# The first pair of FFN1 in an order set by hand: x loaded ahead of the modulation's rows, and two shift columns computed on TensorE

## The chip, the cores and the metric

The kernel is one layer of a latent-token trunk and runs on one core of one Trainium2 chip. The metric is the device time of one execution in microseconds, as the median of several runs. "TensorE", "VectorE", "ScalarE" and "GpSimd" are PE, DVE, ACT and POOL in the profile's rows; SP is the engine whose queue issues nearly all of the DMAs.

## The reference, cut to what matters

The latent stream x (1024 tokens of 1024 channels) and a context stream (256 tokens) go through the same half-step SwiGLU FFN, each modulated by its own conditioning vector:

```python
cond_lat = jax.nn.silu(c)
cond_ctx = jax.nn.silu(c_ctx)[None, :]
m_l = jnp.split(cond_lat @ ada_w[i] + ada_b[i], N_MOD, axis=-1)      # 9 x 1024 columns
m_c = jnp.split(cond_ctx @ ada_w[i] + ada_b[i], N_MOD, axis=-1)
x = x + 0.5 * m_l[2][:, None, :] * swiglu(modulate(rms_norm(x, norm1_w[i]), m_l[0], m_l[1]),
                                          ffn1_w1[i], ffn1_w3[i], ffn1_w2[i])
ctx = ctx + 0.5 * m_c[2][:, None, :] * swiglu(modulate(rms_norm(ctx, norm1_w[i]), m_c[0], m_c[1]), ...)
# modulate(h, shift, scale) = h * (1 + scale) + shift;  swiglu(h) = (silu(h @ w1) * (h @ w3)) @ w2
```

After that come token mixing (retention and gated linear attention), a second half-step FFN and a last norm. All is done in 32-bit floats.

## The kernel before, in words

Channels lie on the 128 partitions: x is eight tiles `x{tg}{k}` of 128 channels by 512 tokens for each of two token groups tg 0 and 1. A 32-bit product is three TensorE matmuls of rounded parts (`mm3`, L62): `hi*hi` (L64), `hi*lo` (L65), `lo*hi` (L66), each 128x128 by 512 columns. The split into the parts is one pass on ScalarE (`hi`, L59) and one subtraction on VectorE or GpSimd (`lo`, L60).

**Modulation.** Column k of one of the nine groups (128 channels) is the dot product of 128 rows of the transposed `ada_w`, an `ada` tile of 128 x 1024 (512 KB), with the cond row, which lies on all partitions. `mod_col` (L101) loads the tile and has VectorE reduce it (L105), once for each stream wanted. A scale column gets `1 +` and the norm's weight in a 128x1 operation (L132). Group 0 is the shift and group 1 the scale of FFN1. There are three places for `ada` tiles (`AB = 3`), shared in turn.

**Norm.** `rstd` squares the eight x tiles on ScalarE, adds them on VectorE (`nacc`, L156), sums over channels on TensorE (L165) and takes the power -0.5 on GpSimd (`nr`, L912). Four diagonal matrices on VectorE (`ndiag`, L175) and four matmuls (L177) spread the result over partitions, and ScalarE copies it to `nrb` (L184). `norm_k` (L187) then makes for each k `nt = x * scale * nrb` on VectorE (L192), `hh` on ScalarE with the shift as bias (L193) and `hl` on VectorE (L194): the two parts of the modulated input.

**The first pair.** `first1` computes the hidden blocks f = 0 and 1 (w1 and w3: four weight columns i = 0 to 3) for both token groups while the norm and the modulation are still being made: stage st takes channel tile k = st of group 0 and k = st - LAG of group 1 (LAG = 4). Columns 2 and 3 of group 0 are held back until k = 3 (`LATE = 4`). In each stage `prep` issues the two modulation columns, the norm of that tile, some of the weights (`FIRST`), the loads of x for group 1 and, at k = 3, the norm's sum of group 1. The weights of this pair are split on ScalarE and GpSimd (eight GpSimd passes). All of this is written once in program order; a scheduler that weighs costs and priorities puts each engine's instructions into their final, fixed order.

**What follows.** Hidden blocks 2 and 3 (`classic_g`), then tiles `t1` to `t4` that are sums of the h tiles (L480 to L497, mostly VectorE), then the other blocks as chains of seven products (`hidden`). The remaining modulation columns are low-priority filler on VectorE (`mods`), each reduced once or twice (latent, context); the list `todo` holds them.

At the start the SP queue issues `cols` (biases and norm weights), the cond row, three `ada` rows, x0, a fourth `ada` row, then x1 to x7.

Of the kernel before, what the change touches and what calls it, by code (L numbers as in the profile page):

```python
# [30 lines left out]
class Trunk:  # L31
# [33 lines left out]
        mm(ps, wa[0], xa[1], start=False, stop=False, skip_group_check=more)  # L65
        mm(ps, wa[1], xa[0], start=False, stop=stop, skip_group_check=more)  # L66

    def consts(self, cond):
        nc, I, cp = self.nc, self.I, self.cp
        self.cols = self.tile(cp, [P, I["cols"].shape[1]], F32, "cols")  # L70
        nc.sync.dma_start(self.cols, I["cols"])
        cond()
# [4 lines left out]
        self.ident = self.tile(cp, [P, P], F32, "ident")  # L77
        self.pad(cp, 16)

    def cond(self):  # L80
        self.mod = [self.tile(self.cp, [P, 72], F32, "modl"), self.tile(self.cp, [P, 40], F32, "modc")]
# [12 lines left out]
    def ada_tile(self):  # L94
        self.ada += 1
        return self.tile(self.dp, [P, D], F32, f"ada{self.ada % AB}")

# [86 lines left out]
        self.nc.scalar.copy(rb[:, :n], pr)  # L184
        return rb[:, :n]

    def norm_k(self, tg, k, a, b, rb, pool, t=None):  # L187
        nc = self.nc
        n = TGS[tg][1]
        t = self.scr(pool, "nt")[:, :n] if t is None else t  # L190
        hi, lo = self.h[tg][k]
        nc.vector.scalar_tensor_tensor(out=t, in0=self.x[tg][k], scalar=a[:, k:k + 1], in1=rb, op0=ALU.mult, op1=ALU.mult)  # L192
        nc.scalar.activation(hi, t, AF.Identity, bias=b[:, k:k + 1])  # L193
        nc.vector.scalar_tensor_tensor(out=lo, in0=t, scalar=b[:, k:k + 1], in1=hi.bitcast(F32), op0=ALU.add,  # L194
                                       op1=ALU.subtract)
        return t

    def norm_t(self, tg, a, b, pool, tp):
# [406 lines left out]
    def first1(self, prep, ws):  # L605
        def first_k(pss, ids, tg, k):
            for i in ids:
                self.mm3(pss[i], self.wslice(ws[i], k), self.h[tg][k], k == 0, k == KD - 1)

        pss = {}  # L610
        prep(0, -1)
        for st in range(KD + LAG):
            if st == 0:
                pss[0] = [self.psA() for _ in range(4)]
            if st == LAG:
                pss[1] = [self.psB() for _ in range(4)]
            for tg, k in ((0, st), (1, st - LAG)):
                if not 0 <= k < KD:
                    continue
                prep(tg, k)  # L620
                late = LATE if tg == 0 else 0
                first_k(pss[tg], range(2) if k < late else range(4), tg, k)
                if k + 1 == late:
                    for kk in range(late):
                        first_k(pss[tg], range(2, 4), tg, kk)
# [635 lines left out]
    def run(self):  # L1261
        nc, tc, I = self.nc, self.tc, self.I
        S = {}

        def opn(name, side="left"):
            S[name] = tc.tile_pool(name=name, bufs=1, reuse_waits="tile", side=side)
            return S[name].__enter__()

        def cls(name):
            S[name].__exit__(None, None, None)  # L1270
# [4 lines left out]
        self.wp = opn("wp")  # L1275
        self.dp = opn("dp", "right")
        xp = opn("xp", "right")
        self.consts(lambda: self.cond())
        self.x, self.h, self.tr = {}, {}, None
        f1 = opn("f1")  # L1280
# [4 lines left out]
        for k in range(MK):  # L1285
            self.mod_col(8 + k, (0,), True)
            self.mod_col(k, (0,), True)
        self.load_x((xp, xp, None), (0,))
        nc.sync.dma_start(self.ident, self.I["ident"])
        self.alloc_h((0, 1), self.hp)  # L1290
        late = [self.tile(self.f1w, [P, D], F32R, f"w{i}") for i in range(1, 5)]
        late = [[(late[2 * i][:, o:o + 512], late[2 * i + 1][:, o:o + 512]) for o in (0, 512)] for i in range(2)]
# [7 lines left out]
        def prep(tg, k):  # L1300
            if k < 0:
                if tg == 0:
                    rb[0] = self.rstd(self.x[0], 512, n1)
                return
            if tg == 0 and k >= MK:
                self.mod_col(8 + k, (0,), True)
                self.mod_col(k, (0,), True)
            self.norm_k(tg, k, self.mcol(1), self.mcol(0), rb[tg], n1)
            if tg == 0:
                for i, q in FIRST.get(k, ()):  # L1310
                    load_first(i, q)
            if tg == 0 and XLK <= k < XLK + 4:
                self.load_x((xp, xp, None), (1,), (2 * (k - XLK), 2 * (k - XLK) + 1))
            if tg == 0 and k == RK:
                rb[1] = self.rstd(self.x[1], 512, n1)
# [21 lines left out]
        xp = opn("xp", "right")  # L1337
# [9 lines left out]
        for i, (tg, k) in enumerate((tg, 4 * q + k) for tg, q in ((0, 0), (1, 1), (0, 1), (1, 0)) for k in range(4)):  # L1347
            o = TGS[tg][0]
# [50 lines left out]
        A = self.bank4(self.psA)  # L1399
# [20 lines left out]
        xp = opn("xp", XS)  # L1420
        self.x = {}
        for tg in LATTG:
            o, n = TGS[tg]
# [25 lines left out]
        late = (None for _ in self.mods_half(f2, (8,)))  # L1449
# [21 lines left out]
MK = 2  # L1471
XLK = 0
RK = 3
LAG = 4
LR = (None, 60)
CRP = 0
VPRI = 100
# [1 line left out]
LATE = 4  # L1479
# [29 lines left out]
def layout(inputs):  # L1509
    g = {k: np.ascontiguousarray(v) for k, v in inputs.items()}  # L1510
    c = np.ascontiguousarray
    A = {}
# [2 lines left out]
    A["c"] = c(g["c"].reshape(1, D))  # L1515
    A["c_ctx"] = c(g["c_ctx"].reshape(1, D))
    A["adaT"] = c(g["ada_w"][0].T).reshape(72, P, D)

    def cols(v):
        return v.reshape(-1, P).T  # L1520
# [31 lines left out]
    j, i = np.arange(P)[:, None], np.arange(P)[None, :]  # L1552
# [30 lines left out]
```

## Time and profile before

| | us |
|---|---|
| median of 3 runs (lowest, highest) | 2210.6 (2210.41, 2212.17) |
| the profiled execution | 2213.09 |
| its span, first to last instruction | 2211.3 |
| TensorE busy in it | 2116.0 |
| VectorE busy in it | 1548.0 |
| ScalarE busy in it | 980.2 |
| GpSimd busy in it | 290.0 |
| first product of the pair starts | 31.55 |

The span is one execution as the profiler saw it, on one core; the profiled execution's own time is a little above it. Rows of the timeline give start, duration, engine, line, operation, what it writes and reads, and in brackets how long the engine had been idle and what ended that.

### The profile page before, as it was taken

The numbers are of one execution on the slowest core, as the hardware profiler recorded it, in microseconds if no ns is written. First come the engines' busy times: TensorE is split into PE (matmuls) and PEld (weight loads), VectorE is DVE, ScalarE is ACT, GpSimd is POOL, SyncE is SP. The second block draws the span as 40 slices with busy tenths as digits, with TensorE's granted clock in tenths as the row PEclk, the third lists the DMA queues.
The fourth block names the chain that finished last, engine by engine and source line by source line (L and its number), as shares of the span: only waits on it lengthen the run. The fifth ranks groups of instructions, "written<-read, shape, count | busy, mean of one in ns | idle before, by whom it ended". The sixth has DMA issues, their size and how long they took to land. (4 is left out here: it accounts for less than half of the span.)

```text
span 2211.3 us, 32718 instructions
## 1 busy us (share of the span) xinstructions
PE 2116.0 (96%) x11442; PEld 1796.9 (81%) x11442; DVE 1548.0 (70%) x2755; ACT 980.2 (44%) x1805; POOL 290.0 (13%) x294
## 2 busy tenths in 40 slices
PE   4999999999999999999989999899999999999998
PEld 3877888887788999887777988788878888888888
DVE  6999999765677755773666546767776767665676
ACT  3324343444454554555553435434344343444553
POOL 2000000000004655431032112200000000010000
PEclk9999999999999999999999999999999999999999
DMA  7548778458886565564222223325134444467674
GB/s 240 173 150 277 220 239 292 154 191 272 271 269 188 158 189 181 177 188 112 88 64 82 73 72 96 95 79 171 58 124 153 162 153 162 144 203 254 207 241 153
DMA packets 203079, 374.44 MB, mean 169 GB/s; under 512 B 23905, under 2 KB 37153, under 8 KB 202913
## 3 DMA queue, kind: packets, MB, share of 16 engines
q1 hardware_dynamic: 202912, 372.34, 52.8%
q8 instruction: 90, 1.47, 0.3%
q14 instruction: 77, 0.62, 0.1%
HBM read 297.76 MB, written 66.09 MB: 165 GB/s over the span
## 5 line engine op out<-in xcount | busy, mean ns | idle before, releaser
L59 ACT ACTIVATE whi<-raw 128x512 fp32r<-128x512 f32 (+1 forms) x659 | 406.3, 623 | 721.8 <-issue 198.8
L60 DVE TENSOR_TENSOR wlo<-raw,whi 128x512 fp32r<-128x512 f32 (+1 forms) x541 | 373.8, 694 | 310.7 <-ACT whi L59 308.2
L64 PE MATMUL psa<-hh,whi 128*128 128x512 f32 (+1 forms) x1476 | 544.6, 370 | 9.4 <-ACT hh L193 6.7
L65 PE MATMUL psa<-hl,whi 128*128 128x512 f32 (+1 forms) x1476 | 544.5, 369 | 1.2 <-DVE hl L60 0.7
L66 PE MATMUL psa<-hh,wlo 128*128 128x512 f32 (+1 forms) x1476 | 543.7, 368 | 1.8 <-DVE wlo L60 1.8
L64 PEld LDWEIGHTS psa<-hh,whi 128*128 128x128 f32 x1476 | 280.6, 190 | 55.4 <-ACT hh L193 7.9
L66 PEld LDWEIGHTS psa<-hh,wlo 128*128 128x128 f32 x1476 | 281.0, 190 | 45.2 <-DVE wlo L60 2.3
L65 PEld LDWEIGHTS psa<-hl,whi 128*128 128x128 f32 x1476 | 280.8, 190 | 45.3 <-DVE hl L60 1.8
L64 PE MATMUL psb<-hh,whi 128*128 128x512 f32 (+1 forms) x696 | 267.1, 385 | 4.7 <-ACT hh L59 2.5
L65 PE MATMUL psb<-hl,whi 128*128 128x512 f32 (+1 forms) x696 | 267.2, 384 | 1.8 <-DVE hl L60 1.8
L66 PE MATMUL psb<-hh,wlo 128*128 128x512 f32 (+1 forms) x696 | 266.7, 383 | 1.0 <-DVE wlo L60 1.0
L60 POOL TENSOR_TENSOR wlo<-raw,whi 128x512 fp32r<-128x512 f32 (+1 forms) x118 | 158.3, 1359 | 201.0 <-ACT whi L59 195.1
L64 PEld LDWEIGHTS psb<-hh,whi 128*128 128x128 f32 x696 | 131.1, 188 | 33.2 <-ACT hh L59 4.7
L65 PEld LDWEIGHTS psb<-hl,whi 128*128 128x128 f32 x696 | 131.3, 189 | 29.0 <-DVE hl L60 3.8
L66 PEld LDWEIGHTS psb<-hh,wlo 128*128 128x128 f32 x696 | 131.3, 189 | 27.5 <-DVE wlo L60 2.3
L912 POOL TENSOR_TENSOR nr<-nr,mhalf 128x4 f32<-128x4 f32 (+1 forms) x11 | 11.6, 1057 | 868.1 <-DVE nr L911 864.4
L60 DVE TENSOR_TENSOR hl<-raw,hh 128x512 fp32r<-128x512 f32 x159 | 111.1, 703 | 16.9 <-ACT hh L59 16.6
L59 ACT ACTIVATE hh<-raw 128x512 fp32r<-128x512 f32 x159 | 97.3, 619 | 20.0 <-DMA raw<-gd 17.0
L65 PE MATMUL psa<-wlo,hh 128*128 128x256 f32 (+1 forms) x320 | 93.3, 291 | 1.6 <-DVE wlo L60 1.6
L64 PE MATMUL psa<-whi,hh 128*128 128x256 f32 (+1 forms) x320 | 93.3, 291 | 1.2 <-ACT s L866 1.2
L66 PE MATMUL psa<-whi,hl 128*128 128x256 f32 (+1 forms) x320 | 92.6, 289 | 0.0
L105 DVE CUSTOM_DVE_ANT_0 junk<-ada,condc,cols 128x1024 bf16<-128x1024 f32 x64 | 82.8, 1294 | 9.6 <-DMA ada<-in_adaT 9.2
(355 smaller groups left out, 3619.2 us busy)
## 6 DMA issues: line engine op xcount, KB each, us to landing
raw<-in_w SPq DMA_DIRECT2D x374, 256.0 KB, 3.1
ada<-in_adaT SPq DMA_DIRECT2D x80, 512.0 KB, 4.4
gd<-s SPq DMA_DIRECT2D x154, 256.0 KB, 2.9
raw<-gd SPq DMA_DIRECT2D x154, 256.0 KB, 3.7
s<-in_w SPq DMA_DIRECT2D x66, 256.0 KB, 4.6
sd<-s SPq DMA_DIRECT2D x44, 256.0 KB, 2.9
hh<-in_w SPq DMA_DIRECT2D x44, 256.0 KB, 4.0
raw<-sd SPq DMA_DIRECT2D x44, 256.0 KB, 3.0
```

Of the source, the lines that this page charges most:

```text
L59: nc.scalar.activation(hi, src, AF.Copy)
L60: (eng or nc.vector).tensor_tensor(out=lo, in0=src, in1=hi.bitcast(F32), op=ALU.subtract)
L64: mm(ps, wa[0], xa[0], start=start, stop=False, skip_group_check=more)
L65: mm(ps, wa[0], xa[1], start=False, stop=False, skip_group_check=more)
L66: mm(ps, wa[1], xa[0], start=False, stop=stop, skip_group_check=more)
L105: nc.vector.tensor_tensor_reduce(out=self.junk, in0=t, in1=self.cs[s], scale=1.0, scalar=self.col("ada_b")[:, j:j + 1], op0=ALU.mult, op1= ...
L912: nc.gpsimd.tensor_tensor(out=r, in0=r, in1=self.mhalf[:, :n], op=ALU.pow)
```

## The change: what it does

1. **Order by hand.** `first1` is written anew and called under a manual schedule for TensorE, VectorE and ScalarE: these three run the pair in the order in which the code stands. SP, GpSimd and the rest of the program are scheduled as before. LAG is 3.
2. **x first.** x of group 0 is issued ahead of the cond row and the `ada` rows; the small constants go through ScalarE's queue. x of group 1 comes in two lots of four, at stages 0 and 1.
3. **Five places** for `ada` tiles instead of three.
4. **Two shift columns on TensorE** (k = 1 and 2, `SH = 2`): `shift_col` loads an untransposed tile `adaN` of the same size and multiplies it with the two cond vectors as columns (`ccol`, 128 x 2), eight matmuls in 32 bits, for both streams at once; ScalarE adds the bias (two 128x1 passes). The columns 1 and 2 of the shift leave the list `todo`.
5. The weights of the pair are split on ScalarE and **VectorE**; GpSimd has no splits there.

```diff
+    def shift_col(self, j):
+        nc = self.nc
+        t = self.ada_tile()
+        nc.sync.dma_start(t, self.I["adaN"][j - 1])
+        o = self.shift[:, 2 * j:2 * j + 2]
+        for k in range(KD):
+            nc.tensor.matmul(o, t[:, k * P:(k + 1) * P], self.ccol[:, 2 * k:2 * k + 2], start=k == 0, stop=k == KD - 1)
+        for s in range(2):
+            nc.scalar.activation(self.mod[s][:, j:j + 1], o[:, s:s + 1], AF.Identity, bias=self.col("ada_b")[:, j:j + 1])
...
+    def first1(self, pools, n1, ws, load_first):
...
+        self.shift = self.psB()
+        acc = self.squares(self.x[0], 512, n1)
+        self.cond()
+        self.mod_col(8, (0,), True)
+        r = self.rstd_col(acc, 512, n1)
+        self.mod_col(0, (0,), True)
+        spread(0, r)
+        acc = None
+        for i, q in FIRST[-1]:
+            load_first(i, q)
+        pss[0] = [self.psA() for _ in range(4)]
         for st in range(KD + LAG):
+            ks = [(tg, k) for tg, k in ((0, st), (1, st - LAG)) if 0 <= k < KD]
+            for tg, k in ks:
+                nt[tg] = self.norm_a(tg, k, a, b, rb[tg], n1)
+            if st + 1 < KD:
+                self.mod_col(9 + st, (0,), True)
+                if st < SH:
+                    self.shift_col(st + 1)
+                else:
+                    self.mod_col(st + 1, (0,), True)
+            if st < 2:
+                self.load_x(pools, (1,), range(4 * st, 4 * st + 4))
+            for tg, k in ks:
+                self.norm_b(tg, k, b, nt[tg])
+            if st < 2:
+                acc = self.squares(self.x[1], 512, n1, "", range(4 * st, 4 * st + 4), acc)
+            for i, q in FIRST.get(st, ()):
+                load_first(i, q)
+            if st == LAG - 1:
+                spread(1, self.rstd_col(acc, 512, n1))
                 pss[1] = [self.psB() for _ in range(4)]
+            for tg, k in ks:
+                products(range(2) if tg == 0 and k < LATE else range(4), tg, k)
+                if tg == 0 and k + 1 == LATE:
+                    for kk in range(LATE):
+                        products(range(2, 4), tg, kk)
...
-            ws[i].append(self.load_half(w[f][:, 512 * q:512 * q + 512], late[i % 2][q] if f else None, nc.gpsimd))
+            ws[i].append(self.half(self.raw_half(w[f][:, 512 * q:512 * q + 512]), late[q] if i == 3 else None))
...
-        self.first1(prep, ws)
+        with tc.manual_schedule(engines={mybir.EngineType.PE, mybir.EngineType.DVE, mybir.EngineType.Activation}):
+            self.first1((xp, xp, None), n1, ws, load_first)
...
-        todo = [(8 * m + k, ctxs) for m, ctxs in EMODS for k in range(KD)]
+        todo = [(8 * m + k, ctxs) for m, ctxs in EMODS for k in range(KD) if m or not 1 <= k <= SH]
...
-AB = 3
+AB = 5
+SH = 2
-LAG = 4
+LAG = 3
-FIRST = {0: ((0, 0), (1, 0)), 1: ((2, 0),), 2: ((3, 0), (0, 1)), 3: ((1, 1), (2, 1)), 4: ((3, 1),)}
+FIRST = {-1: ((0, 0), (1, 0)), 1: ((2, 0),), 2: ((3, 0), (0, 1)), 3: ((1, 1), (2, 1), (3, 1))}
```

`norm_a` is the first two operations of `norm_k`, `norm_b` the third; `products` is the old `first_k`.

How the order moves, at three places. ScalarE from the first copy `nrb` on, before (`nsq` and the second `nacc` are Squares of x of group 1, `w` and `whi` weight halves):

```order
L184 COPY nrb_215<-psb_202 128x512
L155 ACTIVATE nsq_326<-x_90_255 128x512
L59 ACTIVATE w_55_167<-raw_251 128x512
L193 ACTIVATE hh_23_135<-nt_221,modl_80 128x512
L193 ACTIVATE hh_25_137<-nt_247,modl_80 128x512
L155 ACTIVATE nsq_329<-x_91_257 128x512
L155 ACTIVATE nsq_332<-x_99_286 128x512
```

ScalarE from the second `hh` on, in the change (L103 are the 128x1 passes that take a shift column from TensorE's result):

```order
L203 ACTIVATE hh_20_120<-nt_275,modl_88 128x512
L103 ACTIVATE modl_88<-psb_154,cols_78 128x1
L103 ACTIVATE modc_89<-psb_154,cols_78 128x1
L166 ACTIVATE nsq_303<-x_97_294 128x512
L166 ACTIVATE nsq_306<-x_98_296 128x512
L166 ACTIVATE nsq_309<-x_99_298 128x512
L166 ACTIVATE nsq_312<-x_100_300 128x512
```

The Squares of group 1 stood scattered among the other work; now four of them stand in one run behind the second shift column.

TensorE at the start of the products, in the change (before, its products followed the four spreading matmuls without anything between):

```order
L101 MATMUL psb_154<-ccol_80,ada_85_237 128x2 x8
L64 MATMUL psa_226<-hh_18_118,whi_216 128x512
L65 MATMUL psa_226<-hl_19_119,whi_216 128x512
L66 MATMUL psa_226<-hh_18_118,wlo_217 128x512
L64 MATMUL psa_227<-hh_18_118,whi_222 128x512
L65 MATMUL psa_227<-hl_19_119,whi_222 128x512
L66 MATMUL psa_227<-hh_18_118,wlo_223 128x512
L101 MATMUL psb_154<-ccol_80,ada_96_282 128x2 x8
```

Each of the two shift columns stands whole between the products: the first ahead of all of them, the second behind the six of k = 0.

VectorE at stage 2 of the change, where the norm's sum of group 1 enters (before, `nr` of group 1 stood between two reductions):

```order
L202 SCALAR_TENSOR_TENSOR nt_327<-x_12_96,modl_88,nrb_212 128x512
L116 ISA junk_183,modl_88<-ada_109_330,condc_178,cols_78 128x1024
L116 ISA modl_88 128x1
L143 SCALAR_TENSOR_TENSOR modl_88<-modl_88,cols_78 128x1
L116 ISA junk_183,modl_88<-ada_110_334,condc_178,cols_78 128x1024
L116 ISA modl_88 128x1
L208 SCALAR_TENSOR_TENSOR hl_23_123<-nt_327,modl_88,hh_22_122 128x512
L60 TENSOR_TENSOR wl_151<-raw_338,wh_150 128x512
L60 TENSOR_TENSOR wlo_345<-raw_342,whi_344 128x512
L959 TENSOR_SCALAR nr_353<-psb_348 128x4
```

`nr` now stands behind the whole of stage 2 with its two weight splits. From the 196th product to far behind the t tiles TensorE's products stand as before; later some rows are exchanged among neighbours.

More of the change, by code (lines that the diff above doesn't have):

```diff
@@ L66, in mm3, with consts @@
         mm(ps, wa[1], xa[0], start=False, stop=stop, skip_group_check=more)
-    def consts(self, cond):
+    def consts(self):
         nc, I, cp = self.nc, self.I, self.cp
         self.cols = self.tile(cp, [P, I["cols"].shape[1]], F32, "cols")
-        nc.sync.dma_start(self.cols, I["cols"])
-        cond()
+        nc.scalar.dma_start(self.cols, I["cols"])
+        self.ccol = self.tile(cp, [P, 2 * KD], F32, "ccol")
+        nc.scalar.dma_start(self.ccol, I["ccol"])
+        self.ident = self.tile(cp, [P, P], F32, "ident")
+        nc.scalar.dma_start(self.ident, I["ident"])
         self.ones = self.tile(cp, [P, P], F32, "ones")
@@ L76, in consts @@
         nc.vector.memset(self.mhalf, -0.5)
-        self.ident = self.tile(cp, [P, P], F32, "ident")
-        self.pad(cp, 16)
+        self.mod = [self.tile(cp, [P, 72], F32, "modl"), self.tile(cp, [P, 40], F32, "modc")]
     def cond(self):
-        self.mod = [self.tile(self.cp, [P, 72], F32, "modl"), self.tile(self.cp, [P, 40], F32, "modc")]
         self.cs = [self.cond_row("c")]
@@ L185, in rstd, with norm_a @@
         return rb[:, :n]
-    def norm_k(self, tg, k, a, b, rb, pool, t=None):
+    def norm_a(self, tg, k, a, b, rb, pool, t=None):
         nc = self.nc
@@ L603, in first2, with products, spread @@
                 self.c_mul(f, tg, self.H(ws[f, 1], tg))
-    def first1(self, prep, ws):
-        def first_k(pss, ids, tg, k):
-            for i in ids:
-                self.mm3(pss[i], self.wslice(ws[i], k), self.h[tg][k], k == 0, k == KD - 1)
-        pss = {}
-        prep(0, -1)
-        for st in range(KD + LAG):
-            if st == 0:
-                pss[0] = [self.psA() for _ in range(4)]
-            if st == LAG:
-                pss[1] = [self.psB() for _ in range(4)]
[L617 to L625, printed above, removed]
+    def first1(self, pools, n1, ws, load_first):
+        nc = self.nc
+        a, b = self.mcol(1), self.mcol(0)
+        rb, pss, nt = {}, {}, {}
+        def products(ids, tg, k):
+            for i in ids:
+                self.mm3(pss[tg][i], self.wslice(ws[i], k), self.h[tg][k], k == 0, k == KD - 1)
+        def spread(tg, r):
+            pr = self.rstd_rows(r, 512, n1)
+            rb[tg] = self.scr(n1, "nrb")
+            nc.scalar.copy(rb[tg], pr)
+        self.shift = self.psB()
[9 more added lines that the diff above has]
+        pss[0] = [self.psA() for _ in range(4)]
+        for st in range(KD + LAG):
+            ks = [(tg, k) for tg, k in ((0, st), (1, st - LAG)) if 0 <= k < KD]
[17 more added lines that the diff above has]
+                spread(1, self.rstd_col(acc, 512, n1))
+                pss[1] = [self.psB() for _ in range(4)]
+            for tg, k in ks:
[3 more added lines that the diff above has]
+                        products(range(2, 4), tg, kk)
@@ L1277, in run @@
         xp = opn("xp", "right")
-        self.consts(lambda: self.cond())
         self.x, self.h, self.tr = {}, {}, None
+        self.consts()
+        warm = self.tile(self.dp, [P, 8], F32, "warm")
+        nc.scalar.activation(warm, self.mhalf, AF.Silu)
+        self.load_x((xp, xp, None), (0,))
+        nc.scalar.activation(self.ccol, self.ccol, AF.Silu)
         f1 = opn("f1")
@@ L1284, in run @@
         self.psN = self.psB
[L1285 to L1289, printed above, removed]
         self.alloc_h((0, 1), self.hp)
-        late = [self.tile(self.f1w, [P, D], F32R, f"w{i}") for i in range(1, 5)]
-        late = [[(late[2 * i][:, o:o + 512], late[2 * i + 1][:, o:o + 512]) for o in (0, 512)] for i in range(2)]
+        late = [self.tile(self.f1w, [P, D], F32R, f"w{n}") for n in "hl"]
+        late = [tuple(t[:, o:o + 512] for t in late) for o in (0, 512)]
         ws = [[], [], [], []]
```

34 lines of the change are left out of this document (11 added, 23 removed).

## The prediction

> **What bounds the kernel now.** I read the busy shares first, then the windows of 20 us, then the timelines of TensorE and VectorE where those show a loss.
>
> ```profile
> PE 2116.0 (96%) x11442; PEld 1796.9 (81%) x11442; DVE 1548.0 (70%) x2755; ACT 980.2 (44%) x1805; POOL 290.0 (13%) x294
> ```
> TensorE holds the end: 96% of the span. So the question is where its idle time lies, and what else is full there.
>
> ```profile
> 0.00:20.00 20.00, 0.00 (x0) 0.00 (x0) 9.09 (x18) 7.07 (x11) 0.35 (x6) 1.00 0.84 280
> 20.00:40.00 20.00, 12.59 (x40) 9.44 (x40) 15.21 (x20) 7.74 (x14) 9.03 (x6) 1.00 0.67 237
> 40.00:60.00 20.00, 14.47 (x46) 11.07 (x46) 17.27 (x30) 6.13 (x11) 5.00 (x4) 0.67 0.53 172
> 120.00:140.00 20.00, 20.00 (x90) 16.57 (x89) 19.82 (x35) 4.24 (x7) 0.00 (x0) 1.00 0.74 210
> 140.00:160.00 20.00, 16.77 (x65) 12.75 (x64) 18.28 (x31) 7.43 (x13) 0.00 (x0) 0.91 0.31 112
> 160.00:180.00 20.00, 17.38 (x68) 13.53 (x68) 19.15 (x33) 8.70 (x17) 0.00 (x0) 0.91 0.68 224
> 200.00:220.00 20.00, 20.00 (x89) 16.54 (x89) 17.82 (x29) 8.96 (x16) 0.00 (x0) 1.00 0.83 279
> ```
> The columns are TensorE, its weight loads, VectorE, ScalarE and GpSimd (busy us, count), granted clock, DMA share, GB/s. Full speed is 90 products in 20 us. TensorE does nothing for 20 us and little until 60, is full at 120, and loses again from 140 to 180, where VectorE is full too. **There are thus two places**, and the change touches the first; what VectorE does between them decides how much of that arrives.
>
> ```profile
> 21.49 1.87 PE L165 MATMUL psb<-ones,nacc 128*128 128x1 f32 x8 [21.49 <-DVE nacc L156]
> 31.55 1.22 PE L64 MATMUL psa<-hh,whi 128*128 128x512 f32 x2 [2.33 <-ACT hh L193]
> 35.56 0.63 PE L64 MATMUL psa<-hh,whi 128*128 128x512 f32 x1
> 35.99 0.63 PE L65 MATMUL psa<-hl,whi 128*128 128x512 f32 x1
> 36.77 0.40 PE L64 MATMUL psa<-hh,whi 128*128 128x512 f32 x1
> 47.61 1.22 PE L64 MATMUL psa<-hh,whi 128*128 128x512 f32 x2 [3.52 <-ACT hh L193]
> 60.30 0.52 PE L66 MATMUL psa<-hh,wlo 128*128 128x512 f32 x1
> 73.67 0.39 PE L64 MATMUL psb<-hh,whi 128*128 128x512 f32 x1
> 93.39 0.39 PE L64 MATMUL psa<-hh,whi 128*128 128x512 f32 x1
> ```
> By the order of the program the last two are products 109 and 196: 87 products in 19.72 us, 0.2267 each. Without any gap the 196th would have meant a first product at 93.39 - 195 x 0.2267 = 49.2. I call this the **lag**: it grows with every wait of TensorE, and before has 49.2 when the pair ends.
>
> ```profile
> 172.71 0.50 PE L66 MATMUL psa<-hh,wlo 128*128 128x512 f32 x1 [1.83 <-DVE wlo L60]
> 176.69 0.39 PE L64 MATMUL psa<-t1h,whi 128*128 128x512 f32 x1
> ```
> The second is product 517: lag 176.69 - 516 x 0.2267 = 59.7. So 10.5 us are lost at 145 to 177, the last of it to a split on VectorE.
>
> **The change, part by part.** *Start.* x, the cond row and the first scale row (with the small constants) are 2.10 + 0.52 + 0.52 + 0.13 = 3.28 MB ahead of the first reduction.
>
> ```profile
> 0.00:13.30 13.30, 0.00 (x0) 0.00 (x0) 4.30 (x11) 3.17 (x4) 0.35 (x6) 1.00 0.77 237
> 8.43 1.28 DVE L105 CUSTOM_DVE_ANT_0 junk<-ada,condc,cols 128x1024 bf16<-128x1024 f32 x1 [7.43 <-DMA ada<-in_adaT]
> 9.83 1.28 DVE L105 CUSTOM_DVE_ANT_0 junk<-ada,condc,cols 128x1024 bf16<-128x1024 f32 x1
> 16.77 4.67 DVE L156 TENSOR_TENSOR nacc<-nacc,nsq 128x512 f32<-128x512 f32 x6 [1.29 <-ACT nsq L155]
> 23.40 0.16 DVE L911 TENSOR_SCALAR nr<-psb 128x4 f32<-128x4 f32 x1 [1.96 <-PE psb L165]
> 23.93 1.13 ACT L59 ACTIVATE whi<-raw 128x512 fp32r<-128x512 f32 x2
> 24.68 2.70 DVE L175 TENSOR_SCALAR ndiag<-ident,nr 128x128 f32<-128x128 f32 x3 [1.13 <-POOL nr L912]
> 29.87 1.41 DVE L192 SCALAR_TENSOR_TENSOR nt<-x,modl,nrb 128x512 f32<-128x512 f32 x2 [0.90 <-ACT nrb L184]
> 56.81 0.47 DVE L175 TENSOR_SCALAR ndiag<-ident,nr 128x128 f32<-128x128 f32 x2
> 58.40 0.58 ACT L184 COPY nrb<-psb 128x512 f32<-128x512 f32 x1 [0.76 <-PE psb L177]
> ```
> 237 GB/s x 13.3 us = 3.15 MB had moved at 13.3, so I put the first reduction at 13.3 (12 at the 385 GB/s of later windows, 15 if the queue starts slower). The sum of squares is ready by then: adds are 0.80 apart, and eight x tiles precede the row. Reduction and scale take 1.40 (8.43 to 9.83): 14.7. The power on GpSimd and the second reduction run beside each other (1.28, 1.4): 16.1. Two pairs of diagonals at 1.6 less overlap, about 2.8, and the copy, 0.58: 19.5. Two splits of weights stand ahead of the first `nt` on VectorE (two in 1.13 on ScalarE, 0.60 on VectorE after the second): 21.25 against 29.87. First product 1.7 later, at 22.9 against 31.55. **8.6 us earlier.**
>
> *Stages 0 to 2 give most of that back.* Prices, start to start: reduction 1.21 (1.28 less the 0.07 by which neighbours overlap), with scale 1.40; `nt`, `hl` 0.67 (two in 1.41); add 0.80; split 0.60.
>
> ```profile
> L60 DVE TENSOR_TENSOR wlo<-raw,whi 128x512 fp32r<-128x512 f32 x10 | 6.7, 683 | 0.0
> L193 ACT ACTIVATE hh<-nt,modl 128x512 fp32r<-128x512 f32 x16 | 11.3, 720 | 28.5 <-DVE nt L192 17.7 <-DVE modl L105 10.8
> L165 PEld LDWEIGHTS psb<-ones,nacc 128*128 128x128 f32 x16 | 3.7, 330 | 21.7 <-DVE nacc L156 21.5
> 82.39 1.41 DVE L194 SCALAR_TENSOR_TENSOR hl<-nt,modl,hh 128x512 fp32r<-128x512 f32 x2
> ```
> Stage 0: 21.25 + 0.67 + 1.40 + 0.67 = 24.0 for `hl`; three adds, 26.6. Stage 1: 0.67 + 1.40 + 0.75, 29.4. Now a **new wait**. TensorE gets `hl` at 24.0, issues five products at the half-clock spacing of 0.43 (26.15), then the second shift column. The nearest row for that form is the sum of squares: 8 passes in 1.87, 0.234 each. A column is 16 passes: 3.7, done 29.9. ScalarE's two 128x1 copies wait for it, and behind them in its fixed order stand four Squares, behind these VectorE's four adds: 30.3, 30.95, 34.05. (No row has the 128x1 copy; between nothing and a wide pass of 0.6 I take 0.2.) Stage 2: split 0.60, `nt` 0.67, 1.40, second reduction 1.29, `hl` 0.67, two splits 1.2: 39.9. Only then `nr` of the second token group, though its matmuls ended near 36: 41.2, diagonals and copy 3.4, 44.55. Stage 3: `nt` 0.67, 1.40, 1.21, `hl` 0.75: 48.6. There product 20 starts; the 19 before it are done. From here 29 products wait for nothing but weights that are split, and VectorE (5.3 us a stage) stays ahead of TensorE (5.44).
>
> *Clock.*
>
> ```profile
> 50.00:55.00 5.00, 4.80 (x16) 3.59 (x14) 3.00 (x7) 0.44 (x1) 1.84 (x2) 0.50 0.35 115
> 55.00:60.00 5.00, 4.08 (x13) 3.40 (x14) 5.00 (x12) 1.46 (x3) 0.41 (x1) 0.50 0.35 107
> ```
> TensorE was nearly full here and the granted clock stayed 0.50. Stages 0 to 2 of the change are thinner, so I take half speed at 48.6 and for 4 us more, as after 31.55 (0.43 apart until 36.4, 0.23 from 36.77 on): 9.4 products. Lag 52.6 - 28.4 x 0.2267 = **46.2**, 3.0 us better than 49.2. With full clock at once it is 44.3; with 12.7 us at half (47.61 to 60.3 in before), 50.3. The Trainium skill ("TensorE: Matmul & The Clock Gate", What's actually happening) grants full clock after one busy window of about 3.4 us; by that the lag is 45.9. The two rows agree with it only if the narrow matmuls and short gaps in them make a window not busy.
>
> *GpSimd's splits move to VectorE*: eight at 0.60, 4.8 us, counted above where they stand ahead.
>
> ```profile
> 34.23 2.40 POOL L60 TENSOR_TENSOR w<-raw,w 128x512 fp32r<-128x512 f32 x1 [1.81 <-ACT w L59]
> 35.42 1.76 DVE L156 TENSOR_TENSOR nacc<-nacc,nsq 128x512 f32<-128x512 f32 x1
> ```
> An add beside them took 1.76, otherwise 0.69; those losses go, so I use undisturbed prices throughout.
>
> *From the pair to 177.* In the new order VectorE multiplies the first group's gate by product 144 (46.2 + 143 x 0.2267 + 0.2 = 78.8) before the last three norms, each `nt`, `hh`, `hl` in line, 2.2: free for the t tiles at 79.5 + 6.6 = 86.1.
>
> ```profile
> 86.59 1.28 DVE L480 TENSOR_TENSOR t3h<-hh,hh 128x512 f32<-128x512 f32 x2
> 171.97 0.68 DVE L60 TENSOR_TENSOR wlo<-raw,whi 128x512 fp32r<-128x512 f32 x1
> ```
> That is only 0.5 ahead of 86.59, since VectorE idles some 6 us for TensorE. From there to the split that TensorE waits for at 172.71 before has 96 wide operations, 20 reductions and 22 small ones: 57.8 + 24.2 + 2.2 = 84.2, in 86.06 us (1.9 of waits). After: 97, 18 and 20, 82.2. So 86.1 + 82.2 + 1.9 = 170.2 against 172.65: **2.5 us earlier**, two reductions less being most of it (the shift columns serve both streams). Behind that place TensorE's order is nearly the same and the 200 to 220 row shows it full; the 2.5 us reach the end.
>
> Sum: span 2211.3 - 2.5 = 2208.8; the profiled execution 2213.09 - 2.5 = 2210.6. That execution lies 2.5 above the median 2210.6 of the runs, so a median of 2208.1.
>
> **Rivals.** *Faster: the start chain is shorter than my sum.* If the granted clock is full at 48.6 (1.9) and the split at 172 comes before TensorE, so that the 1.83 wait and the nine products at half speed behind it (9 x 0.20) go, it is 2.5 + 1.9 + 1.8 = 6.2, 2204.4. For it: VectorE's whole stream hangs on the lag one to one. Against: VectorE's 82.2 us remain.
>
> *Given back:* the change moves products forward but VectorE's stage sets the end. If the two reductions that are gone are refilled by other filler ahead of the split, only 0.5 is left: 2210.1. For it: VectorE is at 19 to 20 of 20 us in every row from 120 to 180.
>
> *Slower: a shift column costs more than 3.7.* If loads (330 ns) do not overlap matmuls, a pass is about 0.6, not 0.234, a column 9.6 us, and both lie on the chain: the first holds product 1, the second the Squares. That adds 12 us: lag 58, 9 us slower, 2220. It decides from 0.31 us a pass (no gain) and 0.45 (slower by over 4.4). Against: the row of eight passes.
>
> **How the numbers follow.** 0.2% is 4.4 us, about what a measurement of this kernel can tell from no change. Forecast (1 to 4.4 us faster) 0.36, given back 0.18, both within 0.2%; faster 0.32; slower 0.14. The forecast's own range is 2206 to 2210; with the clock's bounds (1.9 down, 4.1 up), the queue's (1.3 down, 1.7 up), the faster rival and the 1.8 us that the runs of before lie apart, 2201.5 to 2213.5.
>
> **What would show it.** First `nt` near 21 and first product near 23; ScalarE idle before its 128x1 copies until near 30; product 20 near 48.6; lag 46 at product 196 and near 57 at product 517. Wrong if a shift column takes over 5 us, if the first scale row lands after 15, or if TensorE no longer waits for VectorE at 145 to 177.

## The result and the profile after

| | before | after |
|---|---|---|
| median of 20 runs each (lowest, highest) | 2211.2 (2206.1, 2217.5) | 2211.6 (2205.7, 2218.4) |
| ratio, 95% interval | | 1.0002 (0.9993 to 1.0011) |
| profiled execution, span | 2211.3 | 2211.6 |

No change that can be measured: between 1.5 us less and 2.4 us more. The predicted 2208.1 lay 3.5 below the median, the median inside the range. In the profile after, product 517 came as much earlier as the forecast said, and still nothing arrived at the end. So the question is where it went.

The start in the profile after, VectorE's timeline (first reduction, first `nt`, adds of group 1, `nr` of group 1):

```profile
14.68 1.28 DVE L116 CUSTOM_DVE_ANT_0 junk<-ada,condc,cols 128x1024 bf16<-128x1024 f32 x1 [2.73 <-DMA raw<-in_w]
...
23.46 0.75 DVE L202 SCALAR_TENSOR_TENSOR nt<-x,modl,nrb 128x512 f32<-128x512 f32 x1
...
33.03 3.08 DVE L167 TENSOR_TENSOR nacc<-nacc,nsq 128x512 f32<-128x512 f32 x4 [1.69 <-ACT nsq L166]
...
41.76 0.15 DVE L959 TENSOR_SCALAR nr<-psb 128x4 f32<-128x4 f32 x1
```

TensorE's timeline of the same profile: the shift columns (L101), the first product, product 20, product 196, the split it waits for, product 517.

```profile
20.86 3.41 PE L101 MATMUL psb<-ccol,ada 128*128 128x2 f32 x16
25.02 0.80 PE L64 MATMUL psa<-hh,whi 128*128 128x512 f32 x1 [0.74 <-ACT hh L203]
...
28.62 3.41 PE L101 MATMUL psb<-ccol,ada 128*128 128x2 f32 x16
...
50.56 0.80 PE L65 MATMUL psa<-hl,whi 128*128 128x512 f32 x1 [2.52 <-DVE hl L208]
...
92.31 0.39 PE L64 MATMUL psa<-hh,whi 128*128 128x512 f32 x1
...
171.85 0.50 PE L66 MATMUL psa<-hh,wlo 128*128 128x512 f32 x1 [1.01 <-DVE wlo L60]
...
174.29 0.40 PE L64 MATMUL psa<-t1h,whi 128*128 128x512 f32 x1
```

ScalarE, the wait that the prediction called new:

```profile
32.06 0.26 ACT L103 ACTIVATE modl<-psb,cols 128x1 f32<-128x1 f32 x1 [2.03 <-PE psb L101]
```

The first product is 6.5 us earlier than 31.55 (8.6 were forecast), product 196 1.1 us earlier than 93.39 (3.0 were forecast), product 517 2.4 us earlier than 176.69. That is the size of the 2.5 of the forecast; how much of it is the change's is looked at under "Why the prediction was right or wrong". But farther down it is gone. The last product that reads a `t` tile, in the profile before and in the one after:

```profile
487.28 0.39 PE L66 MATMUL psb<-t3h,wlo 128*128 128x512 f32 x1
```

```profile
488.36 0.40 PE L66 MATMUL psb<-t3h,wlo 128*128 128x512 f32 x1
```

From 2.4 us ahead to 1.1 us behind, in a stretch where TensorE is full in both and the granted clock is 1.00. No wait took it: TensorE has one wait of note there in each, 1.3 us before and 0.9 after. What took it shows in 24 products in a row, the first and the last (before, then after):

```profile
419.51 0.39 PE L64 MATMUL psa<-t1h,whi 128*128 128x512 f32 x1
...
424.72 0.39 PE L66 MATMUL psa<-t2h,wlo 128*128 128x512 f32 x1
```

```profile
419.44 0.40 PE L64 MATMUL psa<-t1h,whi 128*128 128x512 f32 x1
...
424.81 0.40 PE L66 MATMUL psa<-t2h,wlo 128*128 128x512 f32 x1
```

23 steps take 5.21 us before, 5.37 after: 0.2265 and 0.2335 each. Same operation, same shapes, same clock. The groups by shape from 410 to 480 (count, busy, mean ns of one) say which operand does it, before and after:

```profile
L64 PE MATMUL psa<-hh,whi 128*128 128x512 f32 x32 | 12.4, 389 | 0.0
L64 PE MATMUL psa<-t2h,whi 128*128 128x512 f32 x8 | 3.1, 389 | 0.0
```

```profile
L64 PE MATMUL psa<-hh,whi 128*128 128x512 f32 x32 | 12.5, 390 | 0.0
L64 PE MATMUL psa<-t2h,whi 128*128 128x512 f32 x8 | 3.2, 396 | 0.0
```

Products that read `h` tiles cost what they did; all that read `t1`, `t2`, `t3` tiles became dearer, and there are 648 of them between 138 and 488. Of these, 48 lie ahead of product 517, so behind it an estimate from the two spacings is 600 x 0.0070 = 4.2 us.

Two lines of the change that the diff ahead of the prediction leaves out, because they seemed to do nothing that takes time, are the candidate:

```diff
-        self.pad(cp, 16)
...
+        warm = self.tile(self.dp, [P, 8], F32, "warm")
+        nc.scalar.activation(warm, self.mhalf, AF.Silu)
```

The pad of 64 bytes in the left-hand pool is replaced by `ccol`, which also has 64, so the `h` tiles and the split weights stay where they were. `warm`, 32 bytes a row in the right-hand pool, has no counterpart: every tile that is put below it later moves by 32 bytes: the first x tiles, which TensorE does not read, and the `t` tiles of this FFN. In the kernel before, the `h`, `whi`, `wlo` and `t` tiles all start 128 past a multiple of 256 bytes; in the changed one the `t` tiles start 96 past it.

### The profile page after: what moved, and what is told of

It is laid out like the page before. It is cut to its first block, busy times and chain, and to the rows that moved or that the text cites. A ratio compares the mean times of both kernels' runs of the same rounds, so it can differ in the third digit from the quotient of the medians.

```text
span 2211.6 us, 32785 instructions
## 1 busy us (share of the span) xinstructions
PE 2122.9 (96%) x11474; PEld 1801.7 (81%) x11474; DVE 1540.8 (70%) x2755; ACT 981.6 (44%) x1811; POOL 279.7 (13%) x285
## 5 line engine op out<-in xcount | busy, mean ns | idle before, releaser
L60 POOL TENSOR_TENSOR wlo<-raw,whi 128x512 fp32r<-128x512 f32 (+1 forms) x114 | 152.6, 1359 | 193.3 <-ACT whi L59 187.5
```

The source lines that it names most:

```text
L60: (eng or nc.vector).tensor_tensor(out=lo, in0=src, in1=hi.bitcast(F32), op=ALU.subtract)
```

## The experiments

**1. Is it the place of the tiles?** First the changed kernel with `warm` at 64 bytes, and the kernel before with its right-hand pool moved by 32.

```diff
-        warm = self.tile(self.dp, [P, 8], F32, "warm")
+        warm = self.tile(self.dp, [P, 16], F32, "warm")[:, :8]
```

> The changed kernel with one edit: the small table-warming tile `warm`, first in the right-hand pool, is 16 numbers a row instead of 8, so that every tile behind it, the t tiles of the first FFN among them, starts 32 bytes further on, at a multiple of 64 bytes as in the kernel before. Theory A (addresses): the 648 products that read t tiles are 0.2335 us apart in the changed kernel and 0.2267 before, 0.0067 x 648 = 4.4 us; with the edit they are 0.2267 apart again, product 517 is still near 174, the last product ahead of the gap near 531 comes at 527 to 528.5 instead of 531.9, and the end is 3 to 4.5 us earlier than in the changed kernel (2207 to 2208.6, a ratio near 0.998 to the kernel before). Rival B (the clock or another neighbour of these products slows them): the spacing stays at 0.2335 and the time at 2211.6. Rival C (given back later): the spacing is 0.2267 and the product near 531 comes 3 to 5 us earlier, but waits for loads and splits between 530 and 600 take it, and the end is within 1 us of 2211.6.

```diff
         self.cols = self.tile(cp, [P, I["cols"].shape[1]], F32, "cols")
+        self.pad(self.dp, 8)
```

> The kernel before with one edit: a pad of 8 numbers a row ahead of the other tiles in the right-hand pool, so that the t tiles lie 32 bytes off a multiple of 64, and nothing of the order changes. Theory A: t products 0.2335 apart instead of 0.2267; TensorE is full from 180 to 530 but for one gap of 1.5 near 393, which may absorb some; the last product ahead of the gap near 531 comes 3 to 4.5 us later than 530.8, the end 1.5 to 4.5 us later: 2212.7 to 2215.7. Rival B: spacing and time as before, 2211.2. Rival C: 3 to 4.5 later at 531, but within 1 us of 2211.2 at the end.

The second came as theory A had it: in the order of before, the `t` products are 0.2334 apart as soon as their tiles lie 32 bytes off; 2210.6 against 2209.1 of before on the same chip, ratio 1.0009 (1.0000 to 1.0018). The first did not: at a multiple of 64 bytes they are still 0.2333 apart; 2211.5, ratio 1.0014 (1.0005 to 1.0024). So 64 bytes were not the rule, or it was the chip. Next, `warm` with 32 numbers, which puts the `t` tiles at a multiple of 128 (and of 256):

```diff
-        warm = self.tile(self.dp, [P, 8], F32, "warm")
+        warm = self.tile(self.dp, [P, 32], F32, "warm")[:, :8]
```

> The changed kernel with `warm` 32 numbers a row, so that all tiles behind it start at a multiple of 128 bytes, where all of them start in the kernel before. (With 16 numbers they start at 64 past such a multiple, with 8 at 96.) Theory A2 (products are dearer unless the t tile lies at a multiple of 128 bytes): t products 0.2267 apart, 310 to 310.8 us from product 517 to the last t product near 488 (314.1 in the changed kernel, 313.5 with 16 numbers, 310.6 before), so TensorE is 3 to 3.5 us earlier at 531; if nothing takes that later, the end lies 3 us under the changed kernel and under the run with 16 numbers, a ratio near 0.9985 to before. Rival (something else in the changed right-hand pool makes them dear): 0.2333 apart still. Rival C (later stages take the lead): 3 us earlier at 531, and a ratio of 1.000 to 1.0015 as in those runs.

A miss again: 0.2327, and 314.3 us from product 517 to the last `t` product; 2211.1 against 2211.6, ratio 1.0004 (0.9990 to 1.0018). All variants with dear products had one thing left in common: no `t` tile 128 past a multiple of 256. That made a last pair of theories, tried with the unchanged kernel and two others on one chip:

> The kernel before, unchanged, profiled beside the next two, to see whether the spacing of its t products belongs to the kernel or to the chip and the day. Theory A3 (addresses: in the kernel before, the first FFN's t tiles, the h tiles and the split weights all start 128 past a multiple of 256 bytes; in every variant so far whose t products were 0.2325 to 0.2335 apart, the t tiles started elsewhere, at 0, 64 or 224 past it): 0.2265 to 0.2270 here as in the first profile, and 310.6 us from product 517 to the last t product less what its one gap of 1.5 varies. Theory B (the chip): 0.2325 to 0.2335 here too, and 313 to 314 us.

> The kernel before with a pad of 32 numbers (128 bytes) ahead of the other tiles in the right-hand pool: its t tiles start at a multiple of 256 bytes instead of 128 past it, and nothing else changes. Theory A3: 0.2325 to 0.2332 for t products, some 3 us more from product 517 to the last of them than the unchanged kernel of the same call. Theory B: the same spacing as the unchanged kernel of the same call. Rival A2 (multiples of 128 bytes are enough): 0.2267.

(Where the first text says 224 past the multiple, 96 is right.) The two kernels differ in nothing but a pad of 128 bytes. Groups by shape from 410 to 480, the unchanged kernel and the one with the pad:

```profile
L64 PE MATMUL psa<-hh,whi 128*128 128x512 f32 x32 | 12.5, 389 | 0.0
L64 PE MATMUL psa<-t2h,whi 128*128 128x512 f32 x8 | 3.1, 389 | 0.0
```

```profile
L64 PE MATMUL psa<-hh,whi 128*128 128x512 f32 x32 | 12.5, 389 | 0.0
L64 PE MATMUL psa<-t2h,whi 128*128 128x512 f32 x8 | 3.2, 395 | 0.0
```

389 and 395 ns, 0.2269 and 0.2327 from start to start. It is the place, not the chip. Each of the two was timed only once (2217.0 and 2212.7), so they tell the spacing and nothing of the end. Last, the changed kernel with `warm` moved to the pool of the x tiles, which closes before the `t` tiles are made:

```diff
-        warm = self.tile(self.dp, [P, 8], F32, "warm")
+        warm = self.tile(xp, [P, 32], F32, "warm")[:, :8]
```

> The changed kernel with `warm` (32 numbers) in the pool of the x tiles and nothing else: the change as it was meant, without the shift of the t tiles that came with it. The prediction's step was that the 2.5 us by which product 517 is ahead reach the end. Theory A3: t products 0.2267 apart, 310 to 310.7 us from product 517 to the last t product (314.1 in the changed kernel), the end 2 to 3 us under the kernel before: ratio 0.9985 to 0.9995 (0.9988 with the Squares moved as well). Rival (the start's lead is given back all the same, and only the Squares made the difference): the same spacing, but a ratio of 1.000 to 1.001.

```profile
L64 PE MATMUL psa<-t2h,whi 128*128 128x512 f32 x8 | 3.1, 389 | 0.0
```

389 ns again, and 2207.9 against 2209.5, ratio 0.9993 (0.9981 to 1.0005): on the side forecast, with an interval that still holds no change. All traces together, from product 517 to the last `t` product, less the waits there (one in most, two in some; in the run marked * also less 1.7 for a half-clock stretch at 355):

| `t` tiles past a multiple of 256 bytes | us, each run | spacing |
|---|---|---|
| 128 (before twice, `warm` moved twice) | 309.1, 309.5*, 309.2, 308.6 | 0.2264 to 0.2275 |
| 0 (five kernels; the one without the 48 products, below, is not listed) | 312.8, 312.5, 312.4, 312.4 | 0.2319 to 0.2331 |
| 64 (three kernels) | 312.9, 312.8, 312.9 | 0.2330 to 0.2334 |
| 96 (after, before with 32 bytes) | 313.0, 312.8 | 0.2327 to 0.2337 |

The nine of the lower rows lie 2.9 to 4.4 us above the four of the first, 3.6 by the means. So the place of the tiles is shown to cost TensorE this much between 174 and 488; that the cost reaches the end is a separate question.

**2. Does a lead reach the end at all?** The next run leaves out 48 products; the text below says which:

> Leaves out work: the changed kernel with tiles at multiples of 128 bytes, in which 48 products (the third of each three, low half of the weight, in four of the seven parts of the last three chains of the first FFN, near 440 to 530) are not computed; nothing else changes, their splits and loads stay. 48 x 0.2267 = 10.9 us of TensorE in a stretch where it is full and VectorE half free. If a lead of TensorE at 531 reaches the end (theory: the time behind is set by TensorE's own work, and what I could not see so far is hidden by the scatter of single runs), the end is 10 to 12 us under the run without this cut, near 2198, ratio 0.994 to 0.9955. Rival C (loads, whose rate does not depend on TensorE, set the pace from 531 to 620, or a later stage waits for something else): under half arrives, ratio over 0.997.

```diff
+        cut = self.ncut and (f == NF - 2 or f == NF - 4 and w is self.w3)
...
-                self.mm3(ps, [t[:, k * P:(k + 1) * P] for t in wh], b[k], start and k == 0, k == 3, not start)
+                wk = [t[:, k * P:(k + 1) * P] for t in wh]
+                if cut and wh in (w1, w2, w3, w4):
+                    self.nc.tensor.matmul(ps, wk[0], b[k][0], ...)
+                    self.nc.tensor.matmul(ps, wk[0], b[k][1], ...)
+                else:
+                    self.mm3(ps, wk, b[k], start and k == 0, k == 3, not start)
```

GpSimd's timeline, the fourth `nr` of the program, without the cut (`warm` at 128 bytes) and with it:

```profile
698.68 1.72 POOL L960 TENSOR_TENSOR nr<-nr,mhalf 128x4 f32<-128x4 f32 x1 [4.58 <-DVE nr L959]
```

```profile
686.49 1.72 POOL L967 TENSOR_TENSOR nr<-nr,mhalf 128x4 f32<-128x4 f32 x1 [4.57 <-DVE nr L966]
```

12.2 us ahead at 690; 2197.4 against 2211.6 of before and 2211.1 without the cut, ratio 0.9938 (0.9918 to 0.9957). That is 13.7 us with an interval of 9.5 to 18.1: all of the 10.9 us arrived, and some scatter with it. Rival C falls: a gain of this size that TensorE has by 531 is kept.

**3. The start.** The copies of a shift column behind the Squares, first with `t` tiles at 64, then at 0, then at 128 (with `warm` among the x tiles):

```diff
-                    self.shift_col(st + 1)
+                    copies = self.shift_col(st + 1)
...
                 acc = self.squares(self.x[1], 512, n1, "", range(4 * st, 4 * st + 4), acc)
+                copies()
```

> The changed kernel with t tiles at multiples of 64 bytes, and with the two copies of a shift column on ScalarE behind the four Squares of the same stage, not ahead of them. My theory of the start (the Squares and the adds behind them wait some 2 us for the second shift column, and the second group's chain with them): adds begin 1.7 to 2 us earlier than 33.03, product 20 near 48.7 instead of 50.6, the lag at product 196 near 46.3 instead of 48.1, t tiles near 86.3, the split that TensorE waits for near 172 at 169.4, and so product 517 1.8 us earlier than in the run with the tiles moved alone; at the end 1.8 us earlier where nothing behind takes it. Rival (VectorE's wlo splits and its waits for TensorE near 79 set the t tiles): lag 196 improves, product 517 does not.

> The changed kernel with tiles at multiples of 128 bytes and the shift columns' copies behind the four Squares. The two gains add if TensorE's own order sets the time from 92 to 531: 1.9 us in the start (second group's nr 23.8 us behind the first's, not 25.7) and 3.2 in t products, the last product ahead of the gap near 531 at 524.5 to 526.5 for a first nr at 16.3. If leads reach the end, 5 us under the changed kernel, 2205 to 2208, ratio 0.997 to 0.9985; by rival C within 0.1% of before.

> The changed kernel with the tile `warm` (32 numbers) in the pool of the x tiles, which is closed ahead of the t tiles, and with the shift columns' copies behind the four Squares. The t tiles then start 128 past a multiple of 256 bytes, as before. Theory A3: t products 0.2267 apart and 309.5 to 310.6 us from product 517 to the last t product (312.5 to 313 with the tiles at 0 past it), TensorE 3 us further ahead at 531; with the 1.9 of the Squares, the time 4 to 5 us under the kernel before: ratio 0.9975 to 0.9985. Theory B: 312.5 to 313 us, ratio 0.9985 to 1.0005 as with the Squares alone.

VectorE's adds of group 1 in the first of them:

```profile
31.74 3.07 DVE L167 TENSOR_TENSOR nacc<-nacc,nsq 128x512 f32<-128x512 f32 x4
```

The 1.69 us of idle time ahead of the adds is gone. The first row landed later in this run (first `nr` at 16.95 on GpSimd), so I count from there: the second `nr` comes 23.8 us behind the first, 25.7 with the copies ahead. At least these 1.9 us stay: over the three runs product 517 comes at 167.8 to 170.4, which is 152.7 to 154.4 behind the first `nr`, against 154.8 to 158.0 in the five traces with the copies ahead. At the end: 2210.7, ratio 1.0007 (0.9998 to 1.0015); 2208.9, 0.9985 (0.9971 to 0.9999); and with `t` tiles at 128, 2206.6 against 2209.3, **0.9988 (0.9979 to 0.9997)**, somewhat less than I expected. It is the change with the `t` tiles back in their place and without the wait for the second column; its median is 2.7 us under that of the kernel before (0.7 to 4.6).

No shift columns on TensorE, and three places for rows instead of five:

```diff
-SH = 2
+SH = 0
```

> The changed kernel with t tiles at multiples of 64 bytes, and with no shift column on TensorE: all scale and shift rows are reductions on VectorE again (two more ahead of the first stages, two more for the second stream among the fillers). My theory: in the start chain 2 x 1.21 more on VectorE against the 2.0 us wait for the second column that goes: lag at product 196 near 48.5 (48.1 with the columns); up to the split near 172 another two reductions, 2.4, so that split comes 2.5 to 3 us later than with the columns and product 517 with it; the end 2 to 3 us later than the run with the tiles moved alone. Rival (the columns cost what they save): product 517 and the end within 0.7 us of that run.

```diff
-AB = 5
+AB = 3
```

> The changed kernel with tiles at multiples of 128 bytes and three places for the modulation's rows instead of five. If the rows' loads wait for places in the start (theory: with three a row can only be fetched when the reduction three rows earlier is done, and x and weights stand ahead of it in the queue), VectorE waits for rows in stages 0 to 2, the first product comes 1 to 3 us later and product 196 2 to 5 us later than with five. Rival (five places are not needed, a reduction takes 1.2 and a stage has two): every landmark of the start within 0.5 us.

```profile
32.70 3.08 DVE L167 TENSOR_TENSOR nacc<-nacc,nsq 128x512 f32<-128x512 f32 x4
```

Without the columns no wait stands ahead of the adds, yet they come no earlier, for the two reductions stand there instead: second `nr` 26.2 behind the first (25.7), product 196 77.7 behind it (74.5), product 517 158.5 behind it (156.4, and 156.6 in the mean of the five traces with columns, which lie between 154.8 and 158.0). So the columns are worth about 3 us at product 196 and some 2 at product 517, by a single trace without them. My reason for it was wrong: between the first `t3h` and the split near 172 stand 18 reductions with the columns and 18 without; 20 only in the order of before. The two that the columns save stand ahead of the first `t3h`, 15 against 17. At the end 2211.3 against 2211.5, which tells nothing. With three places product 196 comes 77.1 behind the first `nr`, against 76.0 to 76.1 in the three traces with five places that have a half-clock stretch near 51 as this one has: 1.0 us, less than I thought and not nothing. Product 517, at 157.6, lies within the 154.8 to 158.0 of five places, and the one run of 2216.4 says no more.

**4. Where the scatter comes from.** Runs of one kernel on one chip lie 7 to 15 us apart, lowest to highest. In windows of 750 us, the unchanged kernel of experiment 1 and the one without shift columns:

```profile
690.00:1440.00 750.00, 712.56 (x5073) 639.97 (x5073) 454.93 (x944) 373.53 (x740) 246.27 (x252) 0.98 0.41 122
```

```profile
690.00:1440.00 750.00, 713.65 (x5121) 640.84 (x5120) 461.30 (x954) 379.70 (x754) 249.93 (x254) 1.00 0.41 124
```

The clock column differs, 0.98 and 1.00. From 690 on the clock falls to half for 3.4 us eight times in the one trace, twice in the other, and from the fourth `nr` to the end they take 1518.9 and 1510.1. Over the 206 timed runs, 0.001 of a run's mean granted clock goes with 1.3 us, kernel and chip held fixed. Six stretches more went with 8.8 us here, some 1.5 each, so a lead of 2 us is hardly more than one such stretch; only many runs or landmarks show it.

The traces also show when such a stretch comes. Up to 2190 us, all of them begin and end on one grid of 3.41 us in each trace, and the grid lies elsewhere in most executions. Over all fourteen traces, from 60 us on, the cells of this grid at full clock can be sorted by the share of the cell for which TensorE was busy: under 45%, the next cell was at half clock in 47 of 49 cases; from 45 to 55% in 26 of 59; above that in 8 of 8520. So a wait of the program brings a stretch or not by where the grid happens to lie. This would explain why one program scatters by several stretches; no run here changed the waits to test it.

## Why the prediction was right or wrong

The measured 2211.6 lies in the stated range of 2201.5 to 2213.5, but only because that range is 12 us wide: the gain of 2.5 us that was forecast is not there, and the interval leaves room for 1.5 at most. Two errors of about the size of the forecast stand in the prediction, and both made it too fast.

**The step that failed: "the 2.5 us reach the end".** It rests on 0.2267 for every product, a price that I took from the trace of before and never asked why it is so even. The change moved 648 products to 0.2335, 600 of them behind product 517, and that took 3.6 us of TensorE in the stretch that I called full and therefore safe (3.6 by the means of the table above, 3.9 between the traces before and after). "Given back" was a rival, but by fillers on VectorE; the thing that gave back was a tile of 32 bytes that I had left out of the diff as free. That a lead of 11 us is otherwise kept is shown by the 48 products; for leads of 1 to 3 us it is argued from that, since the scatter hides them in most of the runs.

**The 2.5 itself was mostly luck.** The prediction worked it out for the split on VectorE near 172: 170.2 against 172.65. The product behind that split came at 171.85 instead of 172.71, only 0.9 earlier. The other 1.5 us at product 517 come from a half-clock stretch of 3.4 us at 173.2 that the profile of before has and no other trace has; that it would go was part of the rival "faster", not of the forecast. Product 517 stood at 176.69 in the profile that I worked from. Three more traces of that order have it at 173.0, 171.7 and 172.3 (mean of four 173.4); five of the changed order at 174.3, 171.7, 173.3, 173.2 and 170.0 (172.5). The mean lead is 0.9, and with this spread it is known only to some 3 us either way. The windows from 40 to 60 show another part of the difference; the row of before has a clock of 0.67, the same order with 32 bytes of pad, with 128, and unchanged:

```profile
40.00:60.00 20.00, 14.07 (x55) 10.77 (x55) 19.17 (x32) 6.28 (x11) 4.99 (x4) 0.83 0.59 188
```

```profile
40.00:60.00 20.00, 13.93 (x48) 10.87 (x49) 18.09 (x31) 6.47 (x11) 4.98 (x4) 0.76 0.56 173
```

```profile
40.00:60.00 20.00, 15.29 (x53) 11.99 (x54) 18.10 (x30) 5.99 (x10) 4.99 (x4) 0.74 0.53 169
```

Before has 13.7 us at half clock there, the other three 6.8, 10.2 and 10.2; the excess of 3.4 or more belonged to that one execution and not to the kernel. Put together, lead at 517 and 3.6 for dear products:

| kernel, against before | lead | dear | sum | measured, 95% |
|---|---|---|---|---|
| after | 0.9 | 3.6 | +2.7 | +0.4 (-1.5 to +2.4) |
| `warm` at 64 bytes | 0.9 | 3.6 | +2.7 | +3.1 (+1.1 to +5.3) |
| `warm` at 128 bytes | 0.9 | 3.6 | +2.7 | +0.9 (-2.2 to +4.0) |
| before, 32 bytes off | 0 | 3.6 | +3.6 | +2.0 (0 to +4.0) |
| Squares first, `t` at 64 | 4.1 | 3.6 | -0.5 | +1.5 (-0.4 to +3.3) |
| Squares first, `t` at 0 | 4.1 | 3.6 | -0.5 | -3.3 (-6.4 to -0.2) |
| `warm` moved | 0.9 | 0 | -0.9 | -1.5 (-4.2 to +1.1) |
| `warm` moved, Squares first | 4.1 | 0 | -4.1 | -2.7 (-4.6 to -0.7) |

(Lead with the Squares first: three traces, mean 169.3.) Two of the eight intervals miss the sum, by 0.3 and 0.1 us; where an interval leaves out zero, its sign is that of the sum. The sums carry the uncertainty of the lead, so the table agrees with the account and does not prove it to the microsecond. For the change alone the interval excludes a gain over 1.5 us; the sum would make it a small loss, which the measurement neither shows nor excludes.

**Step by step.** *First reduction 13.3*: 14.7 in the profile after, within the bounds of 12 to 15; 13.3 to 15.3 over the runs of that order, set by when x and the first rows land. *First product 22.9*: 25.0; 1.4 of it from there, most of the rest a wait of 0.90 of the first diagonals for GpSimd's `nr`, which I had hidden behind a reduction. *Shift column 3.7*: 3.41, some 0.213 a pass; the rival at 0.6 a pass falls. *Squares wait for the second column*: shown, 2.03 on ScalarE and 1.69 on VectorE, worth the 1.9 found when they no longer wait. *Three adds, 26.6*: the prices give 26.3 to 26.4; nothing behind rests on it, since the second column sets the next adds. *Product 20 at 48.6*: 50.56, the 2 us of the first steps carried on. *Lag at product 196, 46.2*: 92.31 - 195 x 0.2267 = 48.1, the same 2 us. *VectorE from the first `t3h` to the split, 84.1*: 83.8, from 88.04 to 171.80, with 18 reductions against 20 as counted, for another reason than the one given; so the split's 1.6 us of delay against the forecast are the start's.

*Clock*: 4 us at half behind product 20 were expected. In windows of 5 us of the profile after:

```profile
50.00:55.00 5.00, 4.43 (x13) 3.57 (x14) 5.00 (x8) 1.32 (x2) 0.00 (x0) 0.66 0.95 316
55.00:60.00 5.00, 5.00 (x24) 4.14 (x23) 4.96 (x10) 1.13 (x3) 0.00 (x0) 1.00 0.77 234
```

0.66 over 5 us is 3.4 us at half, then full; two of the five traces of this order have no half-clock stretch behind product 20. The Trainium skill ("TensorE: Matmul & The Clock Gate", What's actually happening), by which one busy window releases the clock, agrees with this run; the 13.7 us of before, with TensorE busy for 4.80 and 4.08 of 5 us in two windows of them, stay unexplained by it.

## What to carry to other kernels

A change that adds or drops even a tiny tile moves every tile behind it: list the start addresses of the operands of the costly products before and after, and compare the spacing of products, not only the waits, for a TensorE without a gap was still 3% slower here, product for product. Take a landmark (the start of one chosen product) from several traces before calling a difference of 2 us a gain; one execution carries its own half-clock stretches. And a gain in a start chain counts only as far as the next place from which on TensorE is full: check it there, then whether it is kept.

## What the hardware showed unexpectedly

A 128x128 by 512 product of 32-bit parts takes 0.2267 us from start to start when its moving tile starts 128 past a multiple of 256 bytes, as the stationary tiles and the `h` tiles did in all kernels here, and 0.2327 (0 past it), 0.2333 (64) or 0.2335 (96) otherwise. Whether the address itself counts or its distance from the weights' was not tried. A 128x128 by 2 product in 32 bits takes 0.213 us a pass, 3.41 us for a column of 1024 rows; this was measured only where the 512-column products beside it are 0.43 apart, about twice their later spacing.

A stretch of half clock followed a 3.41 us cell in which TensorE was busy under 45% of the time in 47 of 49 cases, and a cell in which it was busy for over 55% in 8 of 8520.
